# A hybrid encoder step on one core: small matmuls of the linear attention widened to 128 columns and rows, and the sample tokens' high and low parts in one operand

## The chip, the core and the metric

The kernel runs on one core of a Trainium2 chip. Its engines work side by side, each through its own list of instructions: TensorE (PE, with its weight loads as PEld), VectorE (DVE), ScalarE (ACT), GpSimd (POOL) and SyncE (SP), which here only issues transfers. The metric is device time in microseconds of one execution of the whole step.

## The reference

One layer is computed for 2048 prompt tokens and 32 sample tokens: a normalised and modulated input goes through one projection `z = h @ w_in` to both mixers, a banded softmax attention and a gated linear attention, then gates, an output projection and a gated MLP with a short convolution. What the change touches is the linear attention (4 heads, 64 key and 128 value channels) and the projection of the sample tokens.

```python
log_a = log_sigmoid(gk_low @ w_gk2 + b_gk) / 16
cum = cumsum(log_a within a block); cum_end = its last row
q_t = q * exp(cum) / 8; k_t = k * exp(-cum); k_end = k * exp(cum_end - cum)
att = (q_t k_t^T) * lower_triangle
o = att @ v + q_t @ S
S = exp(cum_end) * S + k_end^T @ v          # from block to block
yb = rmsnorm(o, g_gla) * silu(gb)
```

The reference does it in blocks of 16 tokens; any block length gives the same function.

## The kernel before

Accuracy is kept by splitting operands of the large products into a high and a low part of type f32r, which TensorE takes in one pass: `mm3` (lines 74 to 80) issues high x high, high x low and low x high for each 128 rows of the contraction. Small products of the linear attention are left in plain f32; each such product shows in the trace as two matmuls (two passes).

The input projection has two forms. Transposed pieces (queries, keys, gates) have the weights stationary and 416 tokens moving; they are the "dense stream" below. `n_tile` (line 513) does the values, the swish gate and the decay's low-rank input: 128 tokens (`rows_of`) are the stationary operand, 256 or 272 columns of the weights move. It runs over six column chunks, and in each over 17 token tiles, of which the last, t = 16, holds the 32 sample tokens. Its PSUM tiles `pn` come from a pool of six, ScalarE or VectorE evacuates them to `nx`, and a transfer stores them to `vn`.

The linear attention works in 17 chunks: 16 of 128 prompt tokens and one of the 32 sample tokens, each a generator (`gla_chunk`, line 616) that a loop at the end of its section advances by steps. Heads are taken in pairs p = 0 and 1, with j the head within the pair. In a chunk:

- `gk` is loaded and transposed into `gl` (line 626), whose 17th row is a constant one for the bias; `gl` times `wgk` gives the decay logits in `pz` (line 637, 17 rows of contraction). ScalarE and VectorE turn them into log decays, split in `ah` and `al`.
- per p: matmuls with constant matrices `cm` give the cumulated sums `ex` (lines 660 and 661), ScalarE exponentiates them into `E`, VectorE and GpSimd multiply them into the queries `qd` (tile `qbd`), the keys `kd`, `ke` and `qi`.
- per p: scores into the PSUM tile `pa` (one buffer). A chunk of 128 is cut in three levels: diagonal blocks of 32 (line 698, 128x256), the block of 64 below the diagonal (line 701) and two blocks of 32 (line 703), each of the latter two with 64 stationary columns. Four copies (lines 705 to 709) place them in `at` (tile `att`). `ke` is transposed through `ptk` into `kn` (line 711).
- per p: `po` takes `qi` x state (line 720) and `at` x `vb` (line 724); the state update goes to `pu`, one product per head with 64 stationary columns, on PSUM partitions 0 to 63 and 64 to 127 (line 730), and VectorE adds it to the decayed state `SB` (line 734).
- the norm: ScalarE squares `po` (line 742), takes logarithm and exponential (lines 743 and 744), VectorE finishes the root (lines 745 to 747) and forms `y` in four parts (line 749). Four transpositions of `y` through `pty` (line 754) end the chunk.

TensorE's order is the program's, written out by hand: between the steps of the chunks stand pieces of the dense stream (`pull(qk_stream, n)`, three matmuls of 128x416 each), so that the chains on ScalarE and VectorE have time. From the second p's `po` to `pty` these are six pieces, from the first score product to the second p's four. The order on the other engines in these stages is made by the scheduler that builds the program, and each engine then works strictly in that order. PSUM buffers are few: `pa` and `po` one each, `ex` two, and two that `pz`, `ptk`, `pu` and `pty` share in turn.

```python
            step(cur)
            pull(qk_stream, 2)
            step(nxt)
            pull(qk_stream, 2)
            step(cur)
            pull(qk_stream, 4)
            step(cur)
            step(nxt)
            pull(qk_stream, 3)
            step(cur)
            step(nxt)
            step(after)
            step(load)
            pull(qk_stream, 6 if c < 16 else 1 << 20)
            step(cur)
```

Of the kernel before, what the change touches and what calls it, by code (L numbers as in the profile page):

```python
# [10 lines left out]
F32 = mybir.dt.float32  # L11
F32R = mybir.dt.float32r
U8 = mybir.dt.uint8
AF = mybir.ActivationFunctionType
OP = mybir.AluOpType
# [5 lines left out]
KD = 8  # L21
TP, TS = 2048, 32
# [8 lines left out]
NB = 416  # L31
# [12 lines left out]
def f32(ap):  # L44
    return ap.bitcast(F32)
# [13 lines left out]
def encoder_step(ctx: ExitStack, tc: tile.TileContext, I, O):  # L59
    nc = tc.nc  # L60

    def pool(st, name, bufs=1, **kw):
        return st.enter_context(tc.tile_pool(name=name, bufs=bufs, reuse_waits="tile", **kw))
# [10 lines left out]
    def mm3(out, terms, first=True, last=True):  # L74

        n = len(terms)
        for i, (ah, al, bh, bl) in enumerate(terms):
            nc.tensor.matmul(out, ah, bh, start=first and i == 0, stop=False)  # L78
            nc.tensor.matmul(out, ah, bl, start=False, stop=False)  # L79
            nc.tensor.matmul(out, al, bh, start=False, stop=last and i == n - 1)  # L80
# [88 lines left out]
    hB = []  # L169

    def h_at(x, k, c0, n):
        return hA[x][:, k, c0:c0 + n] if c0 < TA else hB[x][:, k, c0 - TA:c0 - TA + n]
# [65 lines left out]
    with ExitStack() as st:  # L238
        stg = pool(st, "stgA", bufs=2, side="right")
# [5 lines left out]
        pa = pool(ada_st, "ada")  # L245
# [256 lines left out]
        def mod_turn():  # L502
# [7 lines left out]
            for v in range(2, 6):  # L510
                mod_finish(v, 0, KD, p[:, :64].rearrange("p (s v k) -> p v k s", s=2, v=4)[:, v - 2])

        def n_tile(c0, n, w, t):

            m = rows_of(t)
            p = psx.tile([128, 512], F32, name="pn", tag="px")
            mm3(p[:m, :n], [(h_at(0, k, 128 * t, m), h_at(1, k, 128 * t, m), w[0][:, k, :n], w[1][:, k, :n]) for k in range(KD)])
            x = stg.tile([128, 272], F32, name="nx", tag="nx")
            if c0 < 1024:
                nc.scalar.copy(x[:m, :n], p[:m, :n])  # L520
            else:
                nc.scalar.activation(x[:m, :256], p[:m, :256], AF.Sigmoid)
                nc.vector.tensor_mul(x[:m, :256], x[:m, :256], p[:m, :256])
                g2 = gg[:m].unsqueeze(1).to_broadcast([m, 2, 128])
                x2 = x[:m, :256].rearrange("p (a b) -> p a b", a=2)
                nc.gpsimd.tensor_mul(x2, x2, g2)
                if n > 256:
                    nc.vector.tensor_copy(x[:m, 256:n], p[:m, 256:n])
            q_ = nc.scalar if c0 < 1024 else nc.sync
            q_.dma_start(vn[128 * t:128 * t + m, c0:c0 + n], x[:m, :n])  # L530
            if c0 < 512 and t >= 12:
                q_.dma_start(O["v_a"][128 * (t - 12):128 * (t - 12) + m, c0:c0 + n], x[:m, :n])
# [11 lines left out]
        for x, (c0, w0_) in enumerate(n_chunks):  # L544
            n = 272 if c0 == 1280 else 256
            w = wn
# [37 lines left out]
    with ExitStack() as st:  # L584
        stq = pool(st, "stgQ", bufs=2)
        gp = pool(st, "gla")
# [11 lines left out]
        cmf = gp.tile([128, 128], F32, name="cmf", tag="qi0")  # L598
        nc.sync.dma_start(cmf, I["cmask"])
        nc.vector.tensor_copy(cmask, cmf)  # L600
        wgk = gp.tile([17, 256], F32, name="wgk")
        nc.sync.dma_start(wgk, I["wgk"])
        SBP, SBS = [], []
        for p in range(2):
            for x, sb in (("P", SBP), ("S", SBS)):
# [3 lines left out]
        qd = gp.tile([128, 2, 2, 256], F32, name="qbd")  # L609
        nc.vector.memset(qd, 0.0)  # L610
        at = gp.tile([128, 2, 2, 128], F32, name="att")
        nc.gpsimd.memset(at, 0.0)
        gl = gp.tile([17, 128], F32, name="glt")
        nc.vector.memset(gl, 1.0)

        def gla_chunk(c):

            SB = SBS if c == 16 else SBP
            sample = c == 16
            n = rows_of(c)  # L620
# [8 lines left out]
            vb = gp.tile([128, 512], F32, name="vb", tag="vb", bufs=2)  # L629
# [25 lines left out]
            for p in range(2):  # L655
                E = gp.tile([128, 768], F32, name="E", tag=f"E{p}")
# [8 lines left out]
                q, k = qk[:, 0, p, :n], qk[:, 1, p, :n]  # L665
                qi = gp.tile([128, 128], F32, name="qi", tag=f"qi{p}")
                ke = gp.tile([128, 128], F32, name="ke", tag=f"ke{p}")
                kd = gp.tile([128, 256], F32, name="kd", tag=f"kd{p}")
                nc.gpsimd.tensor_mul(kd[:, :n], k, E[:, 640:640 + n])
                for j in range(2):  # L670
                    hs = slice(64 * j, 64 * j + 64)
# [20 lines left out]
            KN = []  # L692
            for p in range(2):

                kd = KD_[p]
                pa = pA.tile([128, 512], F32, name="pa", tag="pa")
                d32 = pa[:n, 0:256].rearrange("p (j c) -> p j c", j=2)[:, :, :n]
                nc.tensor.matmul(d32, kd[:, 0:n], qd[:, p, :, 0:n], start=True, stop=True)
                if not sample:
                    l64 = pa[0:64, 256:384].rearrange("p (j c) -> p j c", j=2)  # L700
                    nc.tensor.matmul(l64, kd[:, 128:192], qd[:, p, :, 128:192], start=True, stop=True)
                    l32 = pa[0:64, 384:512].rearrange("p (j c) -> p j c", j=2)
                    nc.tensor.matmul(l32, kd[:, 192:256], qd[:, p, :, 192:256], start=True, stop=True)
                for j in range(2):
                    nc.vector.copy_predicated(at[:n, p, j, :n], cmask[:n, :n], d32[:, j, :])
                if not sample:
                    nc.scalar.copy(at[0:64, p, :, 64:128], l64)
                    nc.vector.tensor_copy(at[0:32, p, :, 32:64], l32[0:32, :, 0:32])
                    nc.vector.tensor_copy(at[64:96, p, :, 96:128], l32[32:64, :, 32:64])
                pt = pM.tile([128, 512], F32, name="ptk", tag="pm")  # L710
                nc.tensor.transpose(pt[:n, 0:128], KE[p][:, :n], ident)
                kn = gp.tile([128, 128], F32, name="kn", tag=f"kn{p}")
                nc.scalar.copy(kn[:n], pt[:n, 0:128])
                KN.append(kn)
                yield

            po = pO.tile([128, 4, 128], F32, name="po", tag="po")
            for p in range(2):
                E = EX[p]
                nc.tensor.matmul(po[:n, 2 * p:2 * p + 2, :], QI[p][:, :n], SB[p], start=True, stop=False,  # L720
                                 skip_group_check=True)
                for j in range(2):
                    h = 2 * p + j
                    nc.tensor.matmul(po[:n, h, :], at[:n, p, j, :n], vb[:n, 128 * h:128 * h + 128],
                                     start=False, stop=True, skip_group_check=True)

                pu = pM.tile([128, 512], F32, name="pu", tag="pm")
                for j in range(2):
                    h = 2 * p + j
                    nc.tensor.matmul(pu[64 * j:64 * j + 64, 0:128], KN[p][:n, 64 * j:64 * j + 64],  # L730
                                     vb[:n, 128 * h:128 * h + 128], start=True, stop=True)
                for j in range(2):
                    hs = slice(64 * j, 64 * j + 64)
                    nc.vector.scalar_tensor_tensor(SB[p][hs, j, :], SB[p][hs, j, :], E[hs, n - 1:n], pu[hs, 0:128],
                                                   op0=OP.mult, op1=OP.add)
                if p == 0:
                    yield

# [1277 lines left out]
```

## Time and profile before

| | |
|---|---|
| median of 3 runs | 3289.78 us (3287.1 to 3295.14) |
| profiled execution | 3291.58 us, span of its instructions 3289.9 us |
| mean granted TensorE clock | 0.981 |
| stage | row-wise tiles about 160 to 470 us, linear attention about 470 to 790 us |
| matmuls that the change touches in the linear attention | decay 34 matmuls (L637), state update 136 (L730), scores 68 + 64 + 64 (L698, L701, L703) |

How to read it: busy time of TensorE counts a matmul from its start to its modelled end, and neighbours overlap. What a matmul costs in a full stream is the distance between two starts. Weight loads (PEld) run beside matmuls, and an idle time there shows where TensorE's pipeline was interrupted. In a row of the timeline, the first column is the start in us from the span's start, the second the length of the row, then engine, line, operation, `out<-in`, the shape of the weights as rows*columns, the shape of the moving operand, and how many instructions the row holds.

### The profile page before, as it was taken

What the parts mean: (1) busy time and instruction counts of PE and PEld (TensorE: products, weight loads), DVE (VectorE), ACT (ScalarE), POOL (GpSimd) and SP (SyncE); (2) the same over time, 40 slices, a digit from 0 to 9 for tenths busy, and PEclk for the clock granted to TensorE, in tenths of its full rate; (3) what the DMA queues carried; (4) which work ended last, traced back from release to release, by engine and by line L of the source; (5) the groups of instructions that cost most, each with busy time, mean ns of one, the idle gap of its engine ahead of it and who ended that gap; (6) DMA issues with size and microseconds to landing.
All of it is one profiled execution on the core that took longest, in us unless ns stands there. A gap on an engine that the chain in (4) does not pass through costs nothing. (4 is left out here: it accounts for less than half of the span.)

```text
span 3289.9 us, 57758 instructions
## 1 busy us (share of the span) xinstructions
PE 3122.5 (95%) x19928; PEld 2977.8 (91%) x19928; DVE 2267.6 (69%) x4858; ACT 1650.9 (50%) x3835; POOL 579.6 (18%) x687
## 2 busy tenths in 40 slices
PE   6999999999999999999999789999999999999996
PEld 5899998888999999889999689999999999999996
DVE  6725516674555555655676889997788778897876
ACT  4412224443555555533445554565556556575755
POOL 3102101111111111111444523310000001311011
PEclk9999999999999999999999899999999999999998
DMA  7344434545433333665475687687787667878784
GB/s 218 111 126 130 134 114 120 133 119 136 115 105 110 105 110 107 186 199 162 138 210 168 213 250 244 213 249 191 190 221 217 194 192 226 248 245 265 237 264 140
DMA packets 601368, 580.23 MB, mean 176 GB/s; under 512 B 55761, under 2 KB 529570, under 8 KB 601074
## 3 DMA queue, kind: packets, MB, share of 16 engines
q1 hardware_dynamic: 556386, 528.93, 55.0%
q10 hardware_dynamic: 44432, 47.34, 4.5%
q8 instruction: 157, 2.57, 0.3%
q14 instruction: 137, 1.12, 0.1%
q0 software_dynamic: 256, 0.26, 0.0%
HBM read 388.71 MB, written 187.65 MB: 175 GB/s over the span
## 5 line engine op out<-in xcount | busy, mean ns | idle before, releaser
L1616 PE MATMUL ad<-hA,hB 128*128 128x348 f32 (+2 forms) x1791 | 311.3, 324 | 1.2 <-ACT work L1735 0.7
L1616 PEld LDWEIGHTS ad<-hA,hB 128*128 128x128 f32 x1791 | 292.7, 190 | 1.8 <-ACT work L1735 1.0
L78 PE MATMUL pm<-hA,wh 128*128 128x416 f32 x768 | 289.2, 377 | 0.0
L79 PE MATMUL pm<-hA,wh 128*128 128x416 f32 x768 | 270.2, 352 | 0.0
L80 PE MATMUL pm<-hA,wl 128*128 128x416 f32 x768 | 270.0, 352 | 0.0
L1562 DVE TENSOR_TENSOR hA<-raws,hA 128x512 fp32r<-128x512 f32 (+1 forms) x355 | 256.2, 731 | 10.8 <-ACT hA L1559 10.3
L1559 ACT ACTIVATE hA<-raws 128x512 fp32r<-128x512 f32 (+1 forms) x355 | 214.4, 616 | 57.6 <-PE ad L1616 28.6
L1616 PE MATMUL g<-hA,hB 128*128 128x350 f32 (+2 forms) x1044 | 187.1, 329 | 19.4 <-ACT work L1732 17.0
L1562 DVE TENSOR_TENSOR hB<-raws,hB 128x512 fp32r<-128x512 f32 (+1 forms) x271 | 198.5, 736 | 5.5 <-ACT hB L1559 5.4
L938 POOL TENSOR_SCALAR P<-P,mx 128x640 f32<-128x640 f32 (+5 forms) x136 | 101.3, 745 | 548.0 <-DVE mx L937 269.6
L1616 PE MATMUL ad<-hA 128*128 128x350 f32 (+2 forms) x1119 | 195.3, 324 | 1.9 <-DVE hA L1562 1.6
L1616 PEld LDWEIGHTS g<-hA,hB 128*128 128x128 f32 x1044 | 173.2, 193 | 22.6 <-ACT work L1732 19.4
L1616 PEld LDWEIGHTS ad<-hA 128*128 128x128 f32 x1119 | 182.8, 190 | 2.6 <-DVE hA L1562 1.9
L1616 PE MATMUL g<-hA 128*128 128x350 f32 (+2 forms) x975 | 172.9, 327 | 11.4 <-ACT work L1732 6.8
L1559 ACT ACTIVATE hB<-raws 128x512 fp32r<-128x512 f32 (+1 forms) x271 | 165.9, 617 | 34.5 <-PE ad L1616 17.1
L1541 POOL TENSOR_TENSOR raws<-raws 128x512 f32<-128x512 f32 (+1 forms) x69 | 101.0, 1472 | 459.4 <-DMA raws<-in_w_down_dram 307.3
L1616 PE MATMUL ad<-hA,hA 128*128 128x350 f32 (+2 forms) x1020 | 178.5, 324 | 1.0 <-DVE hA L1484 0.5
L78 PE MATMUL pn<-wh,hA 128*128 128x256 f32 (+1 forms) x624 | 178.1, 285 | 0.0
L80 PE MATMUL pn<-wh,hA 128*128 128x256 f32 (+1 forms) x624 | 176.9, 283 | 0.0
L79 PE MATMUL pn<-wl,hA 128*128 128x256 f32 (+1 forms) x624 | 176.8, 283 | 0.0
L1616 PEld LDWEIGHTS g<-hA 128*128 128x128 f32 x975 | 160.1, 191 | 14.4 <-ACT work L1732 7.6
L69 ACT ACTIVATE pth<-pp 128x256 fp32r<-128x256 f32 (+1 forms) x288 | 106.0, 373 | 127.9 <-PE pp L1005 118.0
(439 smaller groups left out, 8995.9 us busy)
## 6 DMA issues: line engine op xcount, KB each, us to landing
raws<-in_w_up_dram SPq DMA_DIRECT2D x220, 256.0 KB, 4.5
raws<-sW SPq DMA_DIRECT2D x176, 256.0 KB, 4.2
sW<-raws SPq DMA_DIRECT2D x88, 256.0 KB, 4.7
raws<-in_w_down_dram SPq DMA_DIRECT2D x80, 256.0 KB, 4.7
wr<-in_w_in_dram SPq DMA_DIRECT2D x76, 256.0 KB, 3.4
sgT<-tx ACTq DMA_DIRECT2D x80, 208.0 KB, 2.7
wa<-in_w_ada_dram SPq DMA_DIRECT2D x64, 256.0 KB, 3.0
keys<-ks SPq DMA_DIRECT2D x128, 128.0 KB, 3.0
```

What stands on the lines that cost most here:

```text
L69: i = nc.scalar.activation(hi, src, AF.Copy)
L78: nc.tensor.matmul(out, ah, bh, start=first and i == 0, stop=False)
L79: nc.tensor.matmul(out, ah, bl, start=False, stop=False)
L80: nc.tensor.matmul(out, al, bh, start=False, stop=last and i == n - 1)
L938: nc.gpsimd.tensor_scalar(P[:m, :tot], P[:m, :tot], mx[:m, 6:7], 1.0, op0=OP.mult, op1=OP.mult)
L1541: getattr(eng, op)(raw(out, n), raw(a, n), raw(b, n))
L1559: nc.scalar.activation(hi[:, :n], raw(i, n), AF.Copy)
L1562: nc.vector.tensor_sub(lo[:, :n], raw(i, n), f32(hi[:, :n]))
L1616: nc.tensor.matmul(out[:, :w], l_[:, k], r_[:, k, :w], start=first and k == 0 and i == 0, stop=k == n - 1 and i == 2, skip_group_check=True)
```

## The change

Four edits, all in what TensorE is given:

- the sample tokens' tile (t = 16) of `n_tile`: high and low parts of the 32 tokens are copied once into `hs`, and 64 columns of it are the stationary operand for both the weights' high and low part. Two matmuls for each of 8 k take the place of three. The two halves of the result are added behind it by a ScalarE copy and a VectorE add. The product low x low is computed too.
- the decay: `wgk` and `gl` have 128 rows, of which `wgk` is zero from row 17 on, so the product has 128 rows of contraction. VectorE clears `wgk` before its load.
- the lower score levels: the two products with 64 stationary columns become one with 128 stationary and 256 moving columns. What is used of it lies on the two diagonal blocks; the copies read there.
- the state update: one product with 128 stationary columns (both heads' keys) and 256 moving columns (both heads' values); of the result the two diagonal blocks are used.

```diff
+        hs = pool(st, "hsmp", side="right").tile([128, KD, 2, TS], F32R, name="hs")
+        for x in range(2):
+            nc.vector.tensor_copy(hs[:, :, x], f32(hB[x][:, :, NB - TS:]))
...
-            mm3(p[:m, :n], [(h_at(0, k, 128 * t, m), h_at(1, k, 128 * t, m), w[0][:, k, :n], w[1][:, k, :n]) for k in range(KD)])
+            if m == 128:
+                mm3(p[:, :n], [(h_at(0, k, 128 * t, m), h_at(1, k, 128 * t, m), w[0][:, k, :n], w[1][:, k, :n])
+                               for k in range(KD)])
+            else:
+
+                for k in range(KD):
+                    for i in range(2):
+                        nc.tensor.matmul(p[:2 * m, :n], hs[:, k].rearrange("p x m -> p (x m)"), w[i][:, k, :n],
+                                         start=k == 0 and i == 0, stop=k == KD - 1 and i == 1)
+                sl_ = stg.tile([128, 272], F32, name="ns", tag="ns", bufs=1)
+                nc.scalar.copy(sl_[:m, :n], p[m:2 * m, :n])
+                nc.vector.tensor_add(sl_[:m, :n], sl_[:m, :n], p[:m, :n])
+                p = sl_
...
-        wgk = gp.tile([17, 256], F32, name="wgk")
-        nc.sync.dma_start(wgk, I["wgk"])
+        wgk = gp.tile([128, 256], F32, name="wgk")
+        nc.vector.memset(wgk, 0.0)
+        nc.sync.dma_start(wgk[:17], I["wgk"])
...
-        gl = gp.tile([17, 128], F32, name="glt")
+        gl = gp.tile([128, 128], F32, name="glt")
...
-                    l64 = pa[0:64, 256:384].rearrange("p (j c) -> p j c", j=2)
-                    nc.tensor.matmul(l64, kd[:, 128:192], qd[:, p, :, 128:192], start=True, stop=True)
-                    l32 = pa[0:64, 384:512].rearrange("p (j c) -> p j c", j=2)
-                    nc.tensor.matmul(l32, kd[:, 192:256], qd[:, p, :, 192:256], start=True, stop=True)
+
+                    low = pa[:, 256:512].rearrange("p (j c) -> p j c", j=2)
+                    nc.tensor.matmul(low, kd[:, 128:256], qd[:, p, :, 128:256], start=True, stop=True)
...
-                    nc.scalar.copy(at[0:64, p, :, 64:128], l64)
-                    nc.vector.tensor_copy(at[0:32, p, :, 32:64], l32[0:32, :, 0:32])
-                    nc.vector.tensor_copy(at[64:96, p, :, 96:128], l32[32:64, :, 32:64])
+                    nc.scalar.copy(at[0:64, p, :, 64:128], low[0:64, :, 0:64])
+                    nc.vector.tensor_copy(at[0:32, p, :, 32:64], low[64:96, :, 64:96])
+                    nc.vector.tensor_copy(at[64:96, p, :, 96:128], low[96:128, :, 96:128])
...
-                for j in range(2):
-                    h = 2 * p + j
-                    nc.tensor.matmul(pu[64 * j:64 * j + 64, 0:128], KN[p][:n, 64 * j:64 * j + 64],
-                                     vb[:n, 128 * h:128 * h + 128], start=True, stop=True)
+
+                nc.tensor.matmul(pu[:, 0:256], KN[p][:n], vb[:n, 256 * p:256 * p + 256], start=True, stop=True)
                 for j in range(2):
                     hs = slice(64 * j, 64 * j + 64)
-                    nc.vector.scalar_tensor_tensor(SB[p][hs, j, :], SB[p][hs, j, :], E[hs, n - 1:n], pu[hs, 0:128],
-                                                   op0=OP.mult, op1=OP.add)
+                    nc.vector.scalar_tensor_tensor(SB[p][hs, j, :], SB[p][hs, j, :], E[hs, n - 1:n],
+                                                   pu[hs, 128 * j:128 * j + 128], op0=OP.mult, op1=OP.add)
```

TensorE's order is otherwise unchanged. Here is its list at the state update of a first p: `po` with the state and with the scores, the update `pu`, then `ex` of the next chunk; sizes are those of the result.

Before:

```order
L720 MATMUL po<-SBP_4984,qi 128x256
L724 MATMUL po<-vb,att 128x128 x2
L730 MATMUL pu<-vb,kn 64x128 x2
L660 MATMUL ex<-cm,ah 128x320
L661 MATMUL ex<-cm,al 128x320
```

After:

```order
L736 MATMUL po<-SBP_4962,qi 128x256
L740 MATMUL po<-vb,att 128x128 x2
L745 MATMUL pu<-vb,kn 128x256
L677 MATMUL ex<-cm,ah 128x320
L678 MATMUL ex<-cm,al 128x320
```

Nothing moved; two products of half height became one.

On VectorE the scheduler made another order of the norm in chunks 3 to 7 and 11 to 14. This is its list in chunk 4, from the state update of the second p to the end of `y`; `ss` are the sums of the norm, and the products into `ke`, `qi` and `qbd` belong to the next chunk.

Before:

```order
L734 SCALAR_TENSOR_TENSOR SBP_4988<-SBP_4988,E,pu 64x128 x2
L627 COPY glt<-pz 16x128
L685 TENSOR_TENSOR ke<-qk,E 128x128
L686 TENSOR_TENSOR qi<-qk,E 128x128
L672 TENSOR_TENSOR qbd<-qk,E 64x128
L745 SCALAR_TENSOR_TENSOR ss_6216<-ss_6216 128x4
L674 TENSOR_TENSOR qbd<-qk,E 64x64
L746 SCALAR_TENSOR_TENSOR ss_6216<-ss_6216 128x4
L675 TENSOR_TENSOR qbd<-qk,E 64x64
L747 SCALAR_TENSOR_TENSOR ss_6216<-ss_6216 128x4
L672 TENSOR_TENSOR qbd<-qk,E 64x128
L749 SCALAR_TENSOR_TENSOR y<-po,ss_6216,sg 128x128 x4
```

After:

```order
L748 SCALAR_TENSOR_TENSOR SBP_4966<-SBP_4966,E,pu 64x128 x2
L644 COPY glt<-pz 16x128
L702 TENSOR_TENSOR ke<-qk,E 128x128
L759 SCALAR_TENSOR_TENSOR ss_6174<-ss_6174 128x4
L703 TENSOR_TENSOR qi<-qk,E 128x128
L760 SCALAR_TENSOR_TENSOR ss_6174<-ss_6174 128x4
L689 TENSOR_TENSOR qbd<-qk,E 64x128
L761 SCALAR_TENSOR_TENSOR ss_6174<-ss_6174 128x4
L691 TENSOR_TENSOR qbd<-qk,E 64x64
L763 SCALAR_TENSOR_TENSOR y<-po,ss_6174,sg 128x128 x4
```

The root of the norm moved ahead of two products, and two products into `qbd` (L692 and the second L689) now stand behind `y`. On ScalarE the logarithm of the norm moved ahead of the first exponential of `ex`, and its exponential ahead of the second, in the same chunks.

## The prediction, made before the changed kernel ran

> **What bounds the kernel now.** I read the page's busy shares first, then busy time in three stretches (the input projection's row-wise tiles from 160 us, the linear attention from 480 us in two pieces), then who waits for whom in the linear attention, and last single matmuls in order of time.
>
> ```profile
> PE 3122.5 (95%) x19928; PEld 2977.8 (91%) x19928; DVE 2267.6 (69%) x4858; ACT 1650.9 (50%) x3835; POOL 579.6 (18%) x687
> ...
> 160.00:470.00 310.00, 305.51 (x2494) 297.10 (x2493) 125.80 (x225) 64.74 (x143) 35.16 (x38) 0.99 0.42 126
> 480.00:640.00 160.00, 158.57 (x881) 134.46 (x880) 110.67 (x385) 71.62 (x247) 22.76 (x54) 1.00 0.50 131
> 640.00:790.00 150.00, 149.41 (x841) 126.22 (x840) 96.64 (x347) 64.27 (x232) 23.06 (x52) 1.00 0.45 117
> ```
>
> The columns of the last three rows are stretch, length, then busy time of PE, PEld, DVE, ACT and POOL, the granted clock and the DMA share. Both stretches that the change touches are TensorE's: it is idle 4.5 us of 310, 1.4 of 160 and 0.6 of 150, at a clock of 0.99 to 1.00. A microsecond less on TensorE is a microsecond less in all, as long as nothing else becomes late. But PE busy overlaps its own pipeline: while it shows 158.6 us of 160, weight loading (PEld) fell from 96% (297.10 of 310) to 84% (134.46 of 160). The waits of PEld between 480 and 790 us say where (total, times, longest):
>
> ```profile
> PEld pa L701 <- issue: 10.3, 31, 0.3
> PEld ex L660 <- issue: 5.3, 31, 0.2
> PEld ptk L711 <- issue: 4.6, 27, 0.2
> PEld pty L754 <- DVE y L749: 2.6, 3, 1.1
> PEld pz L637 <- issue: 3.3, 12, 0.3
> ```
>
> "issue" means that it waited for no other engine. These are the instructions at which the shape of the weights changes: 128 to 64 columns (L701), 64 back to 128 (L660, L711), 128 to 17 rows (L637). I therefore count by starts of matmuls, which hold such gaps, and not by durations. Here is one p of a chunk, from its scores to the next chunk's decay product:
>
> ```profile
> 562.19 0.60 PE L698 MATMUL pa<-qbd,kd 128*128 128x256 f32 x2
> 562.73 0.43 PE L701 MATMUL pa<-qbd,kd 128*64 128x128 f32 x2
> 563.00 0.38 PE L703 MATMUL pa<-qbd,kd 128*64 128x128 f32 x2
> 563.31 0.33 PE L711 MATMUL ptk<-ident,ke 128*128 128x128 f32 x1
> 563.39 0.44 PE L78 MATMUL pm<-hA,wh 128*128 128x416 f32 x1
> 563.67 0.35 PE L79 MATMUL pm<-hA,wh 128*128 128x416 f32 x1
> ...
> 564.42 0.34 PE L80 MATMUL pm<-hA,wl 128*128 128x416 f32 x1
> 564.69 0.69 PE L637 MATMUL pz<-wgk,glt 17*128 17x256 f32 x2
> 565.32 0.46 PE L78 MATMUL pm<-hA,wh 128*128 128x416 f32 x1
> 565.61 0.35 PE L79 MATMUL pm<-hA,wh 128*128 128x416 f32 x1
> ```
>
> The first column is the start. And the same for the state update, with the work before and behind it:
>
> ```profile
> 570.09 0.59 PE L720 MATMUL po<-SBP,qi 128*128 128x256 f32 x2
> 570.52 0.61 PE L724 MATMUL po<-vb,att 128*128 128x128 f32 x4
> 571.06 0.44 PE L730 MATMUL pu<-vb,kn 128*64 128x128 f32 x4
> 571.42 0.41 PE L660 MATMUL ex<-cm,ah 128*128 128x320 f32 x1
> 571.68 0.31 PE L661 MATMUL ex<-cm,al 128*128 128x320 f32 x1
> 571.83 0.31 PE L660 MATMUL ex<-cm,ah 128*128 128x320 f32 x1
> ```
>
> **The change part by part.** Prices where nothing changes shape: a two-pass f32 product of 128x256 takes 0.43 us (L720 to L724, 570.09 to 570.52), a matmul of the dense stream 0.19 (L78 to L80 in every undisturbed row), an ex pair step 0.15 (571.68 to 571.83).
>
> *Lower score levels.* Before: 562.19 to 563.67, 1.48 us from the first score pass to the second dense matmul. After: two 128x256 products, 0.43 + 0.43, the transposition (0.11, priced below at L754) and 0.19, together 1.16. The streamed columns are the same (two products of 128 columns against one of 256), so the 0.32 us are all gap. There are 32 of these:
>
> ```profile
> L701 PE MATMUL pa<-qbd,kd x64: 272/298/324, 489.0 to 764.2; 128*64 128x128 f32 x64
> ```
>
> 64 passes are 32 products, and 272 to 324 ns shows that all look alike. 32 x 0.32 = **10.2 us**.
>
> *Decay.* 564.42 to 565.61 is 1.19 us; without gaps 0.19 + 0.43 + 0.19 = 0.81. 0.38 us in each of 16 chunks: **6.1 us**. The sample chunk I leave out.
>
> *State update.* 570.52 to 571.68 is 1.16; after: four passes of L724 at 0.11 = 0.44, one product 0.43, the ex step 0.15, together 1.02. 0.14 x 32 = **4.5 us**. This is the part with something to lose: the four L730 passes fit in 0.36 us (571.06 to 571.42, a drain at its end included), because the two halves of the array work side by side; one 256-column product needs 0.43. Were the gaps around it to stay, this part would lose 0.07 x 32 = 2.2 us. The Trainium skill, "TensorEngine Tiling (Array Packing)", section Key Properties, has a rule for each side: tiles work in parallel, which speaks for the form before and by itself would make this part the 2.2 us loss, and a change of the tiling mode drains TensorE, which would make it the 4.5 us gain. The trace shows both, in the 0.36 us and in the 0.27 us from L80 to L637 where the stream's step is 0.19.
>
> *Sample tokens.* Six column chunks, 8 k each; three matmuls per k become two.
>
> ```profile
> 466.85 0.28 PE L80 MATMUL pn<-wh,hB 128*128 128x256 f32 x1
> 466.96 0.28 PE L78 MATMUL pn<-wh,hB 128*32 128x256 f32 x1
> ...
> 469.62 0.28 PE L80 MATMUL pn<-wh,hB 128*32 128x256 f32 x1
> 469.73 0.35 PE L78 MATMUL pm<-hA,wh 128*128 128x416 f32 x1
> 469.92 0.35 PE L79 MATMUL pm<-hA,wh 128*128 128x416 f32 x1
> ```
>
> From 466.96 to 469.73 stand 24 matmuls, 0.115 each. 8 fewer in each of 6 tiles: **5.6 us**. In and out of 32 columns no gap shows here (0.11 and 0.19), unlike the f32 products above. 64 columns of this operand type are not in the trace; I take no gap, by the 32 columns as the nearest row, and as the other end the 0.38 us that the decay product loses, in each of 6 tiles: 2.3 us. By the Trainium skill's rule on draining (same page and section), taken to the letter, 32 columns would have gaps too and 64 would cost the same again; the rows show none.
>
> Added work: two copies to hs on VectorE, and in six tiles a ScalarE copy and a VectorE add of 32x256. ScalarE is busy 65 of those 310 us and VectorE 126; six PSUM buffers lie between TensorE and the evacuation, some 14 us of matmuls. I cost them at nothing. Without that cover they are some 1.1 us a tile by L749's 0.28 us for 128 columns (two instructions of 256 columns), 7 us in six. The wgk load now waits on SP's queue for a VectorE memset, and the first gk loads stand behind it. TensorE meanwhile has 33 dense matmuls (6.2 us) before its first transposition of gk, which hides a memset of well under 1 us.
>
> *What is late next.* The four transpositions of y are met just as VectorE finishes y:
>
> ```profile
> 579.37 0.75 PE L754 MATMUL pty<-ident,y 128*128 128x128 f32 x4
> 579.96 0.39 PE L698 MATMUL pa<-qbd,kd 128*128 128x256 f32 x1
> ...
> 578.61 1.13 DVE L749 SCALAR_TENSOR_TENSOR y<-po,ss,sg 128x128 f32<-128x128 f32 x4
> ...
> 723.17 0.60 PE L754 MATMUL pty<-ident,y 128*128 128x128 f32 x4
> 723.61 0.60 PE L698 MATMUL pa<-qbd,kd 128*128 128x256 f32 x2
> ```
>
> At 723 us the four take 0.44 us (0.11 each), at 579 us 0.59: y's last part ended at 579.74, and the last transposition waited 0.15. Over the 16 chunks my count by starts of what stands above 0.44 and the normal step ahead is about 6 us, most of it in five chunks (the three waits of 2.6 us among them). The chain to y starts when po is complete; between that and L754 only the second p's state update gets shorter, by 0.14, so where TensorE waits already this 0.14 comes back as a wait. Against it, in nine chunks (3 to 7 and 11 to 14) the new order puts the logarithm and exponential of the norm one ScalarE step earlier and y ahead of two products into qd on VectorE, which is worth more than 0.15. So: six or seven chunks lose 0.14 each (-0.9), nine gain 0.15 (+1.3), together **+0.4**. The bounds are -2.2 (16 x 0.14, the new order worth nothing) and +6 (all these waits gone).
>
> Two other covers shrink. From the decay product to ex, al has to be made: PE's stretch is shorter by 0.14 + 0.32 and the 0.2 us that L637's end gains, about 0.65. The second scores must wait until the first are copied out of the single PSUM buffer pa:
>
> ```profile
> 564.70 0.22 DVE L709 COPY att<-pa 32x64 f32<-32x64 f32 x1
> 566.55 0.59 PE L698 MATMUL pa<-qbd,kd 128*128 128x256 f32 x2
> ...
> 568.97 0.43 DVE L72 TENSOR_TENSOR al<-u,ah 128x256 fp32r<-128x256 f32 x1 [0.27 <-ACT ah L69]
> ```
>
> Here 1.6 us are left at pa and 2.0 us at ex (569.40 to 571.42); where another split stands in VectorE's queue there is less, and I take 1.5 us of new waits in all, between 0 and 4.
>
> **The sum** against the profiled run's 3291.58 us (span 3289.9): 10.2 + 6.1 + 4.5 + 5.6 + 0.4 - 1.5 = 25.3 us, so 3266.3. That run lies 1.8 us above the median of 3289.78; carried to the median: **3264 us**, 0.8% less. About 0.3% (10 us) is what a measurement of this kernel can tell from no change.
>
> **The rivals.**
>
> *The gaps stay, because they belong to something other than the shape of the weights* (to f32 products next to the single-pass stream, say), so the change does not do what it says. For it: at 32 columns of the sample tiles the shape changes and no gap shows. Against it: L637 and L720 stream the same 256 columns in f32 and differ in rows alone, and take 0.63 (564.69 to 565.32) and 0.43; L720 starts behind the dense stream without a gap. Then 5.6 us remain, less 2.2 for the lost side-by-side work and up to 1 us: 3287.
>
> *VectorE and ScalarE become the bound.* The gaps go, but the waits at L754, ex and pa take a good part: VectorE is busy 69% of the 480 to 640 stretch and works in a fixed order. At the bounds above, 26.4 - 2.2 - 4 - 2.3 = 17.9 is left, and with twice those waits about 12: 3272 to 3278. For it: L754 waits already. Against it: the row at 723 us, and 1.6 to 2 us of cover at the other two places.
>
> *Slower.* The copies out of pa take the path: the wider product fills one PSUM bank over all 128 partitions, and its copies read from partitions 64 to 127 into 0 to 31 and 64 to 95. Before, the copies took from 563.41 to 564.92, 1.5 us; with 1.1 us left after the change, they decide once they take 2.6, and eat the whole gain at 1.65 us a chunk more (26.4 / 16), that is beyond 4.2 us. At 5 us the time would be about 3303. Nothing in the rows makes a copy of the same size three times as long.
>
> **How the numbers follow.** Forecast 75% (3257 to 3272), VectorE-bound 14% (3272 to 3278), gaps stay 7% (about 3287), slower 4%. The forecast's own low end is 26.4 + 6 = 32.4 off 3289.8, 3257, and a microsecond or two for half-clock windows that fall otherwise. The range of 3255 to 3277 takes in most of the second case and leaves out the last two. Faster by over 0.3%: the first two cases, 0.88; within 0.3%: 0.08; slower: 0.04.
>
> **What would show it.** In the changed profile the score product to the second dense matmul should take 1.16 us (1.48 shows the gap rival), the decay stretch 0.81, the last att product to the second ex matmul 1.02 - 0.44 + 0.11 = 0.69; the waits "issue" of PEld at pa and ptk should be gone, and those at ex with them. If L754's waits exceed 8 us, VectorE has become the bound. A gap in front of or behind the 64-column tiles, or a wait for evacuation there, takes from the 5.6 us. The prediction is wrong if the gaps stay, or if the sum holds on TensorE and the end does not move with it.

## The result, and the profile after

| | this | before |
|---|---|---|
| median of 4 runs each | 3270.22 us (3264.53 to 3274.43) | 3288.44 us (3284.61 to 3295.14) |
| ratio | 0.993 (95% interval 0.9913 to 0.9948) | 1 |
| profiled execution | 3270.03 us, span 3268.3, clock 0.979 | 3291.58 us, span 3289.9, clock 0.981 |

The ratio says 23.0 us less, between 17.1 and 28.6 (0.993 of 3288.44, and its ends); the medians are 18.2 apart. The changed kernel was timed twice more, as control of later experiments and against more runs of before: ratios of 0.9936 and 0.9935, medians 21.0 and 20.9 us apart. About 21 us, 0.64%, is the best number for the change.

The busy shares of the page after:

```profile
PE 3098.9 (95%) x19748; PEld 2981.8 (91%) x19748; DVE 2269.5 (69%) x4867; ACT 1654.8 (51%) x3841; POOL 575.0 (18%) x687
```

180 matmuls fewer (48 in the sample tiles, 64 in the scores, 68 in the state updates), and nothing of it shows in the 95%. Where the time went is read by stages. Here are busy times by stretch of before, cut where a stage starts or ends: from the first to the last row-wise tile, linear attention from its first score to its last transposition of y, the attention behind it, and the feed-forward part from its first down product to its last. The columns are stretch, length, then PE, PEld, DVE, ACT, POOL, clock, DMA share and GB/s.

```profile
160.20:469.60 309.40, 304.91 (x2490) 296.52 (x2489) 125.60 (x224) 64.67 (x142) 35.11 (x37) 0.99 0.42 126
488.40:792.00 303.60, 301.57 (x1688) 254.27 (x1686) 202.10 (x713) 132.77 (x470) 43.56 (x100) 1.00 0.46 120
792.00:1844.30 1052.30, 1008.18 (x6664) 952.18 (x6663) 602.98 (x1813) 513.20 (x1434) 259.81 (x334) 0.98 0.49 147
1844.30:3267.80 1423.50, 1363.05 (x8335) 1348.91 (x8335) 1199.72 (x1784) 853.77 (x1591) 188.22 (x154) 0.98 0.76 224
```

The same four stages of the changed kernel:

```profile
161.40:462.50 301.10, 297.69 (x2442) 291.03 (x2441) 127.41 (x228) 67.28 (x147) 33.77 (x36) 1.00 0.42 129
481.80:767.60 285.80, 282.51 (x1554) 261.00 (x1552) 202.44 (x717) 132.31 (x470) 44.05 (x100) 1.00 0.49 128
767.60:1817.80 1050.20, 1004.56 (x6664) 948.71 (x6664) 604.69 (x1815) 513.96 (x1434) 259.47 (x334) 0.98 0.50 147
1817.80:3246.60 1428.80, 1364.98 (x8335) 1351.42 (x8334) 1196.85 (x1783) 854.28 (x1590) 186.74 (x154) 0.98 0.75 222
```

The linear attention is 17.8 us shorter. PEld is at work 261 of its 286 us (91%) instead of 254 of 304 (84%): the interruptions of the pipeline went. The row-wise stage is 8.3 us shorter here. The last stage is 5.3 us *longer*, though nothing in it was changed; more on this below.

The stretch from the prediction, in the changed kernel's timeline of TensorE (first column the start; between fifth and sixth chunk):

```profile
567.59 0.60 PE L715 MATMUL pa<-qbd,kd 128*128 128x256 f32 x2
568.03 0.59 PE L719 MATMUL pa<-qbd,kd 128*128 128x256 f32 x2
568.46 0.27 PE L727 MATMUL ptk<-ident,ke 128*128 128x128 f32 x1
568.49 0.43 PE L78 MATMUL pm<-hB,wh 128*128 128x416 f32 x1
568.76 0.35 PE L79 MATMUL pm<-hB,wh 128*128 128x416 f32 x1
...
569.51 0.35 PE L80 MATMUL pm<-hB,wl 128*128 128x416 f32 x1
569.70 0.59 PE L654 MATMUL pz<-wgk,glt 128*128 128x256 f32 x2
569.95 0.54 PE L78 MATMUL pm<-hB,wh 128*128 128x416 f32 x1
570.32 0.35 PE L79 MATMUL pm<-hB,wh 128*128 128x416 f32 x1
...
574.94 0.61 PE L740 MATMUL po<-vb,att 128*128 128x128 f32 x4
575.38 0.60 PE L745 MATMUL pu<-vb,kn 128*128 128x256 f32 x2
575.63 0.50 PE L677 MATMUL ex<-cm,ah 128*128 128x320 f32 x1
575.96 0.31 PE L678 MATMUL ex<-cm,al 128*128 128x320 f32 x1
```

Scores: 567.59 to 568.76 is 1.17 us (before 1.48). Decay: 569.51 to 570.32 is 0.81 (1.19). State update: 574.94 to 575.96 is 1.02 (1.16), from the first `att` product with its four passes. These are the lengths that the prediction worked out without gaps, to 0.01 us. The longest waits of PEld, by line (total, times, longest), between 473 and 768 us:

```profile
PEld pty L768 <- issue: 2.9, 2, 1.5
PEld pty L768 <- PE pm L80: 1.5, 3, 0.7
PEld ex L677 <- ACT ah L69: 1.1, 2, 0.6
...
PEld pa L715 <- issue: 1.1, 3, 0.6
```

Of the waits put down to "issue" before, the 31 at the lower score product and the 27 at ptk are gone, and of the 31 at ex two are left. What stands at pty is the wait for y, whatever the view names as its end. The sample tile, its entry and its exit:

```profile
460.56 0.28 PE L80 MATMUL pn<-wh,hB 128*128 128x256 f32 x1
460.68 0.28 PE L528 MATMUL pn<-wh,hs 128*64 128x256 f32 x1
...
462.44 0.28 PE L528 MATMUL pn<-wl,hs 128*64 128x256 f32 x1
462.56 0.35 PE L78 MATMUL pm<-hA,wh 128*128 128x416 f32 x1
462.75 0.35 PE L79 MATMUL pm<-hA,wh 128*128 128x416 f32 x1
```

16 matmuls in 1.88 us where 24 took 2.77, with steps of 0.12 and 0.19 at the two ends: no gap at 64 columns of this type. Five of the six tiles lost 0.89 us each and the one with 272 columns 1.0: 5.5 us by starts.

### The profile page after: what moved, and what is told of

Read it like the earlier page. It is cut to its first block, busy times and chain, and to the rows that moved or that the text cites. A ratio compares the mean times of both kernels' runs of the same rounds, so it can differ in the third digit from the quotient of the medians.

```text
span 3268.3 us, 57413 instructions
## 1 busy us (share of the span) xinstructions
PE 3098.9 (95%) x19748; PEld 2981.8 (91%) x19748; DVE 2269.5 (69%) x4867; ACT 1654.8 (51%) x3841; POOL 575.0 (18%) x687
## 5 line engine op out<-in xcount | busy, mean ns | idle before, releaser
L1630 PE MATMUL g<-hA,hB 128*128 128x350 f32 (+2 forms) x1044 | 188.9, 331 | 19.7 <-ACT work L1746 17.1
```

The costliest lines, as they stand in the source:

```text
L1630: nc.tensor.matmul(out[:, :w], l_[:, k], r_[:, k, :w], start=first and k == 0 and i == 0, stop=k == n - 1 and i == 2, skip_group_check=True)
```

## The experiments

### One part of the change at a time

Four kernels, each the kernel before with one of the four edits. They were run once each, beside one run of the kernel before at 3300.16 us, so they are read by stage and not by their totals (3282.13, 3276.97, 3292.07 and 3284.14 us in the order below).

Sample tokens alone:

```
+nc.tensor.matmul(p[:2 * m, :n], hs[:, k]..., w[i][:, k, :n], ...)     # 8 k x 2 in place of mm3
```

> Only the sample tokens' edit. Theory 1 (TensorE sets the pace of the stage, and 64 columns of f32r make no gap): the six tiles t = 16 take 16 matmuls of 0.115 to 0.118 us, so the time from the first row-wise matmul (pn) to the first dense one behind them is 5.5 us shorter than before (309.5 us), give or take a half-clock window of 3.4 us (1.7 us); the linear attention (first score matmul to last y transposition) stays at 303.6 us within 1 us. Rival (the changed order on ScalarE and the added evacuation hold up TensorE): less than 4 us, with waits of TensorE on nx or ns. For the stage behind the attention (first ad matmul to last, 1423.5 us before, 1428.7 in the changed kernel): if its 5 us are chance between executions, this run falls anywhere between 1420 and 1430; if they belong to the edits in the linear attention, it stays within 1.5 us of 1423.5.

Lower score levels alone:

```
-nc.tensor.matmul(l64, kd[:, 128:192], qd[:, p, :, 128:192], ...)
-nc.tensor.matmul(l32, kd[:, 192:256], qd[:, p, :, 192:256], ...)
+nc.tensor.matmul(low, kd[:, 128:256], qd[:, p, :, 128:256], ...)
```

> Only the lower score levels as one product. Theory 1 (the gap belongs to the change of shape): from the first score pass to the second dense matmul behind it 1.17 us instead of 1.47, 32 times, so 9.7 us less in the linear attention (303.6 us before) less what new waits take. Rival (VectorE gives it back): the time from the matmul before the y transpositions to the next score matmul, summed over 16 chunks, grows from 15.7 us to 18 us or more. Row-wise stage unchanged at 309.5 us but for half-clock windows.

State update alone:

```
-for j in range(2): nc.tensor.matmul(pu[64 * j:64 * j + 64, 0:128], KN[p][:n, 64 * j:64 * j + 64], ...)
+nc.tensor.matmul(pu[:, 0:256], KN[p][:n], vb[:n, 256 * p:256 * p + 256], ...)
```

> Only the state update as one product. Theory 1: from the last att product to the second ex matmul 0.69 us instead of 0.83, 32 times, 4.3 us; since what the second p gains lies between po and y, where TensorE waits for VectorE already, 2.2 us of it come back as waits at the y transpositions, unless the new order on VectorE takes them: the linear attention gets 2 to 4 us shorter than 303.6. Rival (side-by-side halves are worth more than the gaps): 0.83 or more, and no gain.

Decay alone:

```
-wgk, gl: 17 rows
+wgk, gl: 128 rows, the others of wgk zero
```

> Only the decay product with 128 rows. Theory 1: from the dense matmul ahead of it to the second one behind it 0.81 us instead of 1.19, 16 times, 6.1 us less in the linear attention (303.6 us) less waits for al at ex of up to 1 us. Rival (the gap belongs to f32 behind f32r, not to 17 rows): 1.0 or more.

The stage that each edit touches, from the windows of the four profiles in the same order (columns as above):

```profile
158.10:458.50 300.40, 297.65 (x2442) 290.98 (x2441) 126.77 (x227) 67.53 (x147) 33.82 (x36) 1.00 0.42 129
```

```profile
485.00:779.50 294.50, 292.46 (x1622) 255.53 (x1621) 203.31 (x713) 131.99 (x470) 43.44 (x100) 1.00 0.47 124
```

```profile
489.20:790.10 300.90, 297.82 (x1618) 257.26 (x1618) 200.16 (x712) 132.68 (x470) 43.93 (x100) 1.00 0.47 121
```

```profile
484.30:782.50 298.20, 295.88 (x1686) 256.45 (x1684) 201.57 (x713) 132.57 (x470) 43.63 (x100) 1.00 0.47 122
```

Against 303.6 us of before, the linear attention is 9.1 us shorter with the scores alone, 2.7 with the state update alone, 5.4 with the decay alone: 17.2 together, against 17.8 of the whole change. The parts add up; none needs another. With the sample tokens alone that stage did not move (303.73 us), and the row-wise stage was 9.0 shorter, more than the 5.5 within 1.7 that had been expected. By starts the six tiles have 5.5 of it, and TensorE's only wait for an evacuation in that stage is one of 0.4 us. The rest is scatter: the nine profiles with this edit have 300.4 to 304.1 us there (mean 302.7), the four without it 306.4 to 309.7 (mean 308.1), 5.3 apart.

Each part takes away its own waits only. With the state update alone, PEld still waits at pa 32 times; with the scores alone it still waits at ex. Two rows, of the state update alone and of the scores alone:

```profile
PEld pa L701 <- issue: 10.6, 32, 0.3
```

```profile
PEld ex L660 <- issue: 5.3, 31, 0.2
```

The state update's 2.7 us are less than its gap. Counted by starts over its 32 places, the stretch of the state update fell from 27.0 to 22.8 us, 4.2 less. In the same kernel the four transpositions of y, counted from the matmul ahead of them to the next score product, grew from 15.8 to 17.0 us over 16 chunks: 1.1 us came straight back as waits for y.

### The shape or the number of products?

The two narrow score products became one, so the gain could come from one product less. The changed kernel, with the lower levels as two products of 64 columns each that keep all 128 stationary columns:

```
-nc.tensor.matmul(low, kd[:, 128:256], qd[:, p, :, 128:256], start=True, stop=True)
+for c0 in (0, 64):
+    nc.tensor.matmul(low[:, :, c0:c0 + 64], kd[:, 128:256], qd[:, p, :, 128 + c0:192 + c0], start=True, stop=True)
```

> The changed kernel, but the lower levels in two products again, each with all 128 stationary columns and 128 moving columns (two heads x 64). As many products and streamed columns as before, no change of shape. Theory 1 (the gap belongs to the change of shape): four passes at 0.11 us, so 1.17 us from the first score pass to the second dense matmul, as in the changed kernel (1.17), and the linear attention at 285.9 us within 1. Rival (the gap belongs to the number of separate small products): 1.3 or more, and 4 us or more on the linear attention.

Its timeline at the place in the changed kernel's timeline above:

```profile
571.24 0.60 PE L715 MATMUL pa<-qbd,kd 128*128 128x256 f32 x2
571.67 0.61 PE L720 MATMUL pa<-qbd,kd 128*128 128x128 f32 x4
572.12 0.27 PE L729 MATMUL ptk<-ident,ke 128*128 128x128 f32 x1
572.14 0.43 PE L78 MATMUL pm<-hB,wh 128*128 128x416 f32 x1
572.41 0.35 PE L79 MATMUL pm<-hB,wh 128*128 128x416 f32 x1
```

571.24 to 572.41 is 1.17 us, the same as with one product, where before two products of the same streamed size, with 64 stationary columns, took 1.48. The time was 3269.76 us (one run). The gap belongs to the shape of the weights.

Nor is a narrow product slow in itself. Single starts in the trace before (medians over the 32 places) put the gap where the shape changes: from the last pass with 128 columns and 256 streamed to the first with 64 the step is 0.31 us where 0.22 is normal, then 0.16, 0.11 and 0.11 from one narrow pass to the next, where 0.11 is also the step of the same streamed size at 128 columns, and 0.20 back to 128.

### How much do the waits for y hold back?

TensorE has six pieces of the dense stream between the second p's `po` and `pty`. If that cover is what is short, one or two pieces more there, taken from the three pieces ahead of the step before, should take the waits away. `pull7` and `pull8` are the changed kernel with

```
-pull(qk_stream, 3)
+pull(qk_stream, 2)                       # pull8: 1
...
-pull(qk_stream, 6 if c < 16 else 1 << 20)
+pull(qk_stream, 7 if c < 16 else 1 << 20)   # pull8: 8
```

and the changed kernel itself ran beside them.

> The changed kernel with one piece of the dense stream (three matmuls, 0.57 us) moved from ahead of the second p's po to ahead of the y transpositions. Theory 1 with the waits at y as the one place where VectorE still holds up TensorE (17.1 us summed from the matmul ahead to the next score matmul, 10.0 without waits): those fall by 0.5 us in five to seven chunks, so the linear attention is 2.5 to 4 us shorter than 285.9. Rival (VectorE is the bound of a chunk, a wait moves elsewhere): less than 1 us shorter, with new waits at po, ex or pa.

> As pull7 with two pieces moved (1.13 us), one piece left ahead of the second p's po. Theory 1: the waits at y shrink by up to 1.1 us in the three chunks that wait longest, 3.5 to 6 us less in the linear attention than 285.9; at ex, which follows sooner on ScalarE's exponentials, no wait above 1 us in sum. Rival: the second ex waits for ScalarE to free its PSUM buffer, and nothing is gained over pull7.

> The changed kernel once more, for a second profile and more times. If what the profile lost behind the attention (1428.7 us from first to last ad matmul against 1423.5) is chance between executions, this length falls anywhere between 1420 and 1430 while the linear attention stays at 285.9 within 1 and the row-wise stage at 301 within 2; the time is 21 to 25 us below before. If the loss belongs to the change, 1427 to 1430 again and a time 16 to 20 us below before.

| five runs each | median | ratio to before (95%) | transpositions of y by starts, 16 chunks | linear attention |
|---|---|---|---|---|
| changed | 3270.2 us | 0.9936 (0.9924 to 0.9949) | 16.5 us | 285.7 us |
| pull7 | 3269.19 us | 0.9934 (0.9922 to 0.9947) | 13.7 us | 282.6 us |
| pull8 | 3263.5 us | 0.9922 (0.9908 to 0.9936) | 11.8 us | 281.1 us |

(The changed kernel's first profile gives 16.5 too.) Without any wait the transpositions are 0.62 us a chunk, 10.0 in all. pull7 takes 2.7 and pull8 4.6 us of the 6.5 us of waits away, and the stage gets shorter by 3.1 and 4.6. So the waits for y do reach the end of their stage. At the end of the kernel the medians are 1.0 and 6.7 us below the changed kernel's, with ratios whose intervals overlap. TensorE's waits for y in pull8's profile between 480 and 765 us (total, times, longest) are down to one row with one wait, where the changed kernel has three:

```profile
PE pty L768 <- DVE y L763: 0.9, 1, 0.9
```

Here is one of the three in the changed kernel's timeline; what a row waited for, and how long, stands in brackets:

```profile
532.61 0.35 PE L80 MATMUL pm<-hB,wl 128*128 128x416 f32 x1
534.07 1.01 PE L768 MATMUL pty<-ident,y 128*128 128x128 f32 x4 [1.11 <-DVE y L763]
```

The last dense matmul starts at 532.61, the first transposition 1.46 us later, where the stream's step is 0.19.

The pieces did not act as cover alone, though. For pull7 0.5 us less was expected in each of five to seven chunks. By starts chunk 0 (counted from 0) lost 1.7 us, chunk 8 1.0 and chunk 12 0.35; chunks 1, 2 and 9 kept their waits, and chunk 10 waits 0.25 longer. In the chunks that wait longest, two stores of the dense stream's queries or keys, which ScalarE issues (ACTq in the view), stand in its list ahead of the squares of `po`. Here is chunk 1 in the changed kernel, where the last `att` product starts at 511.14 us, and then in pull7, where it starts at 511.63:

```profile
510.56 1.10 ACTq L211 DMA_DIRECT2D ks<-qh  x2
511.71 0.28 ACT L756 ACTIVATE y<-po 128x128 f32<-128x128 f32 x1 [1.18 <-PE po L740]
```

```profile
511.61 1.10 ACTq L211 DMA_DIRECT2D ks<-qh  x2
512.76 0.28 ACT L756 ACTIVATE y<-po 128x128 f32<-128x128 f32 x1 [1.18 <-PE ex L678]
```

In both the squares start 0.05 us behind the end of the two issues (issuing is not counted as busy, so the bracket puts that time down to TensorE). They start 0.56 us behind the `att` product in the changed kernel and 1.13 in pull7: the piece's 0.57 us came back in the chain. In chunks 0 and 8 of pull7 the stores no longer stand ahead, and the squares start 0.31 us behind that product instead of 1.55 and 1.13; in pull8 all four squares follow at once in every chunk but 2 and 10. What the moves gained is cover and ScalarE's order together, and no run moved only one of the two.

### The same cure elsewhere

The attention's sample unit has the same kind of narrow f32 product: five transpositions of P with 32 rows and five products with 64 columns of `vr`, once for each of 8 heads. The kernel is pull8 with all 128 rows and columns in the first four of each five (the rows of P behind the 32 tokens set to zero, the other head's columns of `vr` computed and not used):

```
+if sample: nc.gpsimd.memset(P[:, :512], 0.0)
-nc.tensor.transpose(pp_[:kn, 0, :TS], P[:TS, 128 * kt:128 * kt + kn], ident[:TS, :TS])
+nc.tensor.transpose(pp_[:, 0, :], P[:, 128 * kt:128 * kt + 128], ident)        # kt < 4
-py[:64, :TS] from vr[:, kt, 64 columns]
+py[:, :TS] from va[:, kt, 128 columns]
```

pull8 and the changed kernel ran beside it.

> pull8, and in the sample units of the attention the transpositions of P take all 128 rows (rows 32 to 127 are cleared by GpSimd first) and the products with the values take 128 stationary columns (both heads' values, of which one half is used); the last key tile of 32 rows stays as it is. Theory 1 (the gap belongs to the change of shape, anywhere): from the last y transposition to the first ad matmul 8 us less than pull8's 1047.5 us, give or take 3 us for half-clock windows, and the whole 25 to 40 us below before. Rival (these units wait for their chain on VectorE, ScalarE and GpSimd anyway, or the clearing stands in GpSimd's queue): within 3 us of pull8.

> pull8 once more beside the other two: if the 4.7 us that the linear attention gained over the changed kernel (281.1 against 285.8) reach the end, its median is 3 to 7 us below the changed kernel's in the same rounds; if they are lost behind the attention, within 2 us of it.

> The changed kernel in the same rounds, 21 us below before give or take 4; linear attention 285.8 within 1; first to last ad matmul between 1420 and 1430.

PEld's waits between 764 and 1500 us, at these transpositions and at the products, in pull8:

```profile
PEld pp L1011 <- issue: 7.5, 27, 0.3
...
PEld py L1038 <- issue: 4.4, 16, 0.3
```

and in the kernel with the wide products:

```profile
PEld py L1044 <- issue: 2.2, 8, 0.3
PEld pp L1017 <- issue: 2.2, 8, 0.3
```

L1017 is the fifth transposition, left narrow, and 8 waits at each line are one for each head: only the narrow step's are left. The stretch from the end of the linear attention to the feed-forward part, by windows, pull8 first, then with the wide products:

```profile
763.90:1811.40 1047.50, 1005.74 (x6665) 950.61 (x6665) 603.93 (x1812) 512.81 (x1432) 259.28 (x334) 0.98 0.50 147
```

```profile
763.50:1804.00 1040.50, 998.30 (x6665) 954.55 (x6664) 605.00 (x1813) 515.38 (x1434) 262.11 (x342) 0.98 0.50 149
```

The stretch is 7.0 us shorter with as many matmuls (5.8 against pull8's second profile, 1046.3 us). The attention alone, from the last transposition of y to the last `py`, is 719.4 us against 729.7, and 728.8 to 734.1 in all twelve profiles without the wide products. The medians are 3260.88 us (ratio 0.9906, 0.9893 to 0.992), 3263.99 for pull8 (0.9923, 0.9908 to 0.9939) and 3269.18 for the changed kernel (0.9935, 0.9923 to 0.9947). By the medians the wide products are worth 3.1 us at the end, at the edge of the 3 us named for the rival, and the ranges of single runs overlap (3251.12 to 3262.52 against 3259.35 to 3273.31): in the stage the gain is shown, at the end its size is not. Likewise pull8 is 6.7 and 5.2 us below the changed kernel by the medians of the two sets, and the intervals of their ratios overlap. The kernel with both is the fastest version found, 0.9% below the kernel before (0.8 to 1.1%).

## Why the prediction was right

The forecast case happened, and at each of the places named beforehand. Of its sum of 25.3 us:

- **Lower score levels, 10.2.** By starts over 32 places the stretch lost 9.7 us; alone, the edit shortened its stage by 9.1. The median stretch is 1.47 us before and 1.17 after: 0.30 a place where the one shown gave 0.32.
- **Decay, 6.1.** 5.8 by starts, 5.4 alone in its stage.
- **State update, 4.5.** 3.9 by starts in the whole change, 4.2 alone. The side-by-side work of two 64-column halves was given up at some 0.07 us a place (0.36 against 0.43) and the gaps around it, an estimated 0.21 (these 0.07 and the 0.14 won), went with it: the shape change outweighs the parallel halves, as chosen.
- **Sample tokens, 5.6.** 5.5 by starts of the six tiles. No gap at 64 columns, as taken from the row with 32. The bound of 2.3 with a gap falls.
- **Waits at y, +0.4.** This step had the wrong sign: transpositions by starts went from 15.8 to 16.5 us, -0.7. Both halves of "six or seven chunks lose 0.14 each (-0.9), nine gain 0.15 (+1.3)" can be followed in the trace. Of the nine with the new order, in the eight 3 to 7, 11, 13 and 14 y now ends 4.75 us behind the start of the last `att` product (5.17 in most of them before) and nothing waits; that half holds, but for chunk 12, whose y is 1.0 us later than before (5.18 against 4.14) and which now waits 0.35. The nine together won 0.9. But in the long-waiting chunks 0, 1, 2, 8 and 9 the waits went from 4.3 to 5.7 us, 0.29 each and not 0.14: in four of them the chain to y itself became 0.15 to 0.2 us longer, with ScalarE's squares of `po` starting 1.55 us behind the last `att` product in chunks 0 and 2, before 1.46 and 1.37, and its logarithm 0.19 later in 1 and 9. I had shortened TensorE's cover and kept the chain's length. The chain does not start when po is complete there, as the prediction has it: in these five chunks ScalarE's stores, shown above for chunk 1, stand ahead of the squares.
- **Other new waits, -1.5.** The terms at their places come to 9.7 + 5.8 + 3.9 - 0.7 = 18.7 us, and the stage got 17.8 shorter: 0.9 us for all others, among them one wait at pa.

17.8 and 5.5 are 23.3 us, 2.0 less than the forecast sum of 25.3: the first five terms fell 2.6 short, the waits at y alone 1.1, and the other waits cost 0.6 less. At the end about 21 arrived. The forecast of 3264 us is 6 us below the measured median of 3270.2: these 2.0, some 2 between the stages and the end, and what medians of four runs scatter.

What the agreement hides is the stage behind. The profiled run of the changed kernel gave back 5.3 us in a stage without any edit. This stage took 1420.3 to 1426.2 us in the five profiles without the whole change, 1422.6 to 1428.7 in the eight with it, and the extremes go with how long the clock stood at half speed in it, 34.5 us of 1420.3, 53.2 of 1428.7; between them the order does not hold (47.4 us of 1428.5, 49.5 of 1424.5). The signs named beforehand disagree: the changed kernel's second profile, in `changed_again`, gave 1428.5 us again, as it should if the loss belongs to the change, but a time 21 us below before, as it should if it is chance; its third gave 1426.8. The kernel with the sample tokens alone gave 1425.9, beyond the 1.5 us around 1423.5 that it should have kept if the loss came from the linear attention. The attention and its projection in between, without an edit too, was 2 us shorter in the changed kernel, 5.5 in its second profile. These were not predicted; whether 2 or 3 us of them belong to the change, by where it puts the end of the attention against the clock's steps, stays open. No experiment here moved only that.

The rivals:

- *The gaps stay.* Fell at all three places (1.17, 1.02, 0.81 us), and `low_two` shows the shape as the cause for the scores.
- *VectorE and ScalarE become the bound.* Fell. The sign named for it was waits at y above 8 us; they are 6.5 (16.5 less the 10.0 without waits), 0.7 more than before. But the mechanism is there in part, since pull8 took 4.6 us out of them.
- *Slower, by the copies out of pa.* Fell. PE's own waits in the linear attention of the changed kernel:

```profile
PE pty L768 <- DVE y L763: 2.7, 3, 1.1
PE pa L715 <- DVE att L725: 0.3, 1, 0.3
```

One wait of 0.3 us at pa. The copies that now read from partitions 64 and above are hardly slower than before:

```profile
L724 DVE COPY att<-pa x32: 218/219/221, 484.0 to 742.1; 32x64 f32<-32x64 f32 x32
L725 DVE COPY att<-pa x32: 228/228/230, 484.2 to 742.3; 32x64 f32<-32x64 f32 x32
```

219 and 228 ns in the middle, against 211 and 219 before.

## What to carry to other kernels

In a stage that TensorE fills, count by starts of matmuls, and look for idle weight loads that wait for nothing: small two-pass f32 products with fewer than 128 stationary columns or rows cost here 0.14 to 0.38 us a place more than the same product padded to 128 by 128, as long as the padding adds no streamed columns in all. What TensorE gains shortens the cover of every chain beside it, so the next step is to give the chain that is met first more independent work, as pull8 did with two pieces of the dense stream, and to see what stands ahead of that chain in its engines' lists. When pricing that, let the chain's own length move too: the order on the other engines changes with TensorE's.

## What was not expected of the hardware

- Whether a narrow shape costs a gap depends on the kind of product. With f32r operands (one pass), 32 and 64 stationary columns went in and out of the 128-column stream at steps of 0.11 to 0.19 us, no longer than without a change of shape. With plain f32 (two passes), 64 columns and 17 rows cost 0.14 to 0.38 us a place. The number of passes is not all of it: the transposition of gk, one pass of plain f32 with 16 columns, showed no gap (0.48 us from the dense matmul ahead of it to the second behind it, at 475.78 us of before, and 0.19 + 0.11 + 0.19 without one), while the transposition of P, one pass with 32 rows, started 0.28 us behind the dense matmul in pull8 and 0.19 with all 128 rows. No f32r product with few rows was looked at. Why they differ was not tried. Nor are these passes alike: one of the two of a 256-column f32 product takes 0.22 us, an f32r matmul of 256 columns 0.115.
- A stage without any edit varied by 8 us between profiles of these kernels (1420.3 to 1428.7 us), with 34.5 to 53.2 us of half clock in it. A single profile pair can therefore not settle a difference of a few us at the end; the stage that an edit touches, which repeated within 1 us (285.9 and 285.7, 286.0 us in three profiles of the changed kernel; 281.1 twice for pull8), can.
